# Two result buffers and a third for the last tile, with two-tile bodies, in a 2x2 average pool

## The chip, the cores and the metric

The kernel runs on one core of one Trainium2 chip. The metric is the device time of one execution in microseconds (us). Before the change it was 3103.94 us (median of six runs, 3103.81 to 3104.12). A program on one core has no second core or die to compare with.

## The reference

```python
# x: float32 [32, 128, 256, 256], kernel_size 2, stride 2 -> float32 [32, 128, 128, 128]
for i in range(h_out):
    for j in range(w_out):
        window = x[:, :, 2*i:2*i+2, 2*j:2*j+2]
        output[:, :, i, j] = np.mean(window, axis=(2, 3))
```

1.07 GB are read and 0.27 GB written, and there are three additions and one multiplication for each output.

## The kernel before

An output row is made of two neighbouring input rows, 512 numbers. A tile is 32 such pairs of rows on each of 128 partitions: 8 MB in (64 KB a partition), 2 MB out (16 KB a partition). There are 127 whole tiles, and one last tile that is cut into four parts (meant to keep the end of the run short). Four engines share the work:

- SyncE issues loads into two input buffers.
- VectorE adds the two rows of each pair (the first add, in place), then neighbouring columns (the second add, into a result buffer).
- ScalarE multiplies by 0.25 in place, tells SyncE that the input buffer is free, and issues the store.
- The DMA engines do the loads and stores.

Every dependence is a semaphore by hand. `take(engine, sem, n)` waits for `n` and takes it away again. The core of the program (cut; comments added here):

```python
TILE = 32
OUTS = 4
# ... ins: 2 tiles [128, 32, 512]; res: OUTS tiles [128, 32, 128]
def tile_sum(b, o, first=False):
    it, dst = ins[b], res[o]
    take(dve, loaded[b], 16)
    dve.tensor_add(out=it[:, :, 0:w], in0=it[:, :, 0:w], in1=it[:, :, w:]).then_inc(ready)
    if not first:
        take(dve, stored[o], 16)          # the store of four tiles back
    take(dve, ready)
    dve.tensor_add(out=dst, in0=it[:, :, 0:w:2], in1=it[:, :, 1:w:2]).then_inc(summed)

def tile_scale(b, o, done):
    take(act, summed)
    act.sem_inc(free[b])                  # SyncE may load into this input buffer
    act.mul(out=res[o], in_=res[o], mul=0.25).then_inc(done)

def tile_store(t, o):
    take(act, scaled)
    act.dma_start(out=ot[t], in_=res[o]).then_inc(stored[o], 16)
# ... the first four tiles of VectorE and ScalarE are written out, then a loop of four tiles a pass,
# ... then three tiles written out, then the four parts of the last tile
```

Of the kernel before, what the change touches and what calls it, by code (L numbers as in the profile page):

```python
# [9 lines left out]
@with_exitstack  # L10
def kernel(
    ctx: ExitStack,
    tc: tile.TileContext,
    x: bass.AP,
    kernel_size: bass.AP,
    stride: bass.AP,
    out: bass.AP,
):
    nc = tc.nc
    P = nc.NUM_PARTITIONS  # L20

    n, c, h, w = x.shape
    k = int(kernel_size)
    s = int(stride)
    h_out = (h - k) // s + 1
    w_out = (w - k) // s + 1
    R = n * c * h_out
    units = R // P if R % P == 0 else 0


    if k == 2 and s == 2 and h % 2 == 0 and w == 256 and units >= 1024:
        _pool_2x2(ctx, tc, x, out, units)
    else:
        _generic_pool(ctx, tc, x, out, k, s, n, c, h, w, h_out, w_out)


TILE = 32
OUTS = 4


def _pool_2x2(ctx, tc, x, out, units):
    nc = tc.nc
    P = nc.NUM_PARTITIONS
    f32 = mybir.dt.float32
    w = x.shape[3]
    w_out = w // 2
    sp, act, dve = nc.sync, nc.scalar, nc.vector

    xv = x.rearrange("n c (ho a) w -> (n c ho) (a w)", a=2)
    ov = out.rearrange("n c ho wo -> (n c ho) wo")  # L50

    in_pool = ctx.enter_context(tc.tile_pool(name="inp", bufs=2))
    out_pool = ctx.enter_context(tc.tile_pool(name="outp", bufs=OUTS))
    ins = [in_pool.tile([P, TILE, 2 * w], f32, name="in_tile") for _ in range(2)]
    res = [out_pool.tile([P, TILE, w_out], f32, name="res") for _ in range(OUTS)]

    loaded = [ctx.enter_context(nc.semaphore(f"loaded{b}")) for b in range(2)]
    free = [ctx.enter_context(nc.semaphore(f"free{b}")) for b in range(2)]
    summed = ctx.enter_context(nc.semaphore("summed"))
    scaled = ctx.enter_context(nc.semaphore("scaled"))  # L60
    stored = [ctx.enter_context(nc.semaphore(f"stored{b}")) for b in range(OUTS)]
    tail = ctx.enter_context(nc.semaphore("tail"))
    ready = ctx.enter_context(nc.semaphore("ready"))
    held = ctx.enter_context(nc.semaphore("held"))



    def take(engine, sem, n=1):
        engine.wait_ge(sem, n)
        engine.sem_inc(sem, -n)  # L70

    def block(r0, g):
        rows = slice(r0, r0 + g * P)
        return xv[rows].rearrange("(p g) f -> p g f", p=P), ov[rows].rearrange("(p g) f -> p g f", p=P)

    whole, rest = divmod(units - 1, TILE)
    rest += 1
    xt = xv[0:whole * TILE * P].rearrange("(t p g) f -> t p g f", p=P, g=TILE)
    ot = ov[0:whole * TILE * P].rearrange("(t p g) f -> t p g f", p=P, g=TILE)
    loops, left = divmod(whole - OUTS, OUTS)  # L80

    def tile_load(t, b):
        sp.dma_start(out=ins[b], in_=xt[t]).then_inc(loaded[b], 16)

    def tile_sum(b, o, first=False):
        it, dst = ins[b], res[o]
        take(dve, loaded[b], 16)
        dve.tensor_add(out=it[:, :, 0:w], in0=it[:, :, 0:w], in1=it[:, :, w:]).then_inc(ready)  # L88
        if not first:
            take(dve, stored[o], 16)  # L90
        take(dve, ready)
        dve.tensor_add(out=dst, in0=it[:, :, 0:w:2], in1=it[:, :, 1:w:2]).then_inc(summed)  # L92

    def tile_scale(b, o, done):
        take(act, summed)
        act.sem_inc(free[b])
        act.mul(out=res[o], in_=res[o], mul=0.25).then_inc(done)  # L97

    def tile_store(t, o):
        take(act, scaled)  # L100
        act.dma_start(out=ot[t], in_=res[o]).then_inc(stored[o], 16)

    parts, a = [], 0
    while a < rest:
        b = rest if rest - a <= 4 else a + (rest - a) // 2
        parts.append((a, b))
        a = b

    psem = [ctx.enter_context(nc.semaphore(f"part{k}")) for k in range(len(parts))]

    with tc.tile_critical():

        for b in range(2):
            tile_load(b, b)
        with sp.Fori(2, 2 + 2 * ((whole - 2) // 2), 2) as i:
            for b in range(2):
                take(sp, free[b])
                tile_load(i + b, b)
        t = 2 + 2 * ((whole - 2) // 2)
        while t < whole:  # L120
            take(sp, free[t % 2])
            tile_load(t, t % 2)
            t += 1



        take(sp, free[whole % 2])
        it, dst = ins[whole % 2], res[whole % OUTS]
        for (a, b), s in zip(parts, psem):
            sp.dma_start(out=it[:, a:b], in_=block((whole * TILE + a) * P, b - a)[0]).then_inc(s, 16)  # L130
        take(sp, held)
        sp.dma_start(out=ot[whole - 1], in_=res[(whole - 1) % OUTS]).then_inc(stored[(whole - 1) % OUTS], 16)


        for o in range(OUTS):
            tile_sum(o % 2, o, first=True)
        with dve.Fori(0, loops) as i:
            for o in range(OUTS):
                tile_sum(o % 2, o)
        for o in range(left):  # L140
            tile_sum(o % 2, o)
        take(dve, stored[whole % OUTS], 16)
        for (a, b), s in zip(parts, psem):
            take(dve, s, 16)
            dve.tensor_add(out=it[:, a:b, 0:w], in0=it[:, a:b, 0:w], in1=it[:, a:b, w:]).then_inc(ready)  # L145
            take(dve, ready)
            dve.tensor_add(out=dst[:, a:b], in0=it[:, a:b, 0:w:2], in1=it[:, a:b, 1:w:2]).then_inc(summed)  # L147


        for t in range(OUTS):  # L150
            tile_scale(t % 2, t, scaled)
            tile_store(t, t)
        with act.Fori(OUTS, OUTS + loops * OUTS, OUTS) as i:
            for o in range(OUTS):
                tile_scale(o % 2, o, scaled)
                tile_store(i + o, o)
        for t in range(OUTS + loops * OUTS, whole):
            tile_scale(t % 2, t % OUTS, scaled if t < whole - 1 else held)
            if t < whole - 1:
                tile_store(t, t % OUTS)  # L160
        act.sem_inc(free[(whole + 1) % 2], -1)
        for a, b in parts:
            take(act, summed)
            act.mul(out=dst[:, a:b], in_=dst[:, a:b], mul=0.25).then_inc(scaled)  # L164
            take(act, scaled)
            act.dma_start(out=block((whole * TILE + a) * P, b - a)[1], in_=dst[:, a:b]).then_inc(tail, 16)


        take(sp, tail, 16 * len(parts))
        for o in range(OUTS):  # L170
            if o != whole % OUTS:
                take(sp, stored[o], 16)


def _generic_pool(ctx, tc, x, out, k, s, n, c, h, w, h_out, w_out):
# [92 lines left out]
```

## Time and profile before

| | before |
|---|---|
| time, median of 6 | 3103.94 us |
| VectorE busy | 54% |
| ScalarE busy | 15% |
| DMA, 40 slices | nine tenths or more in each |
| moved over the span | 433 GB/s |

From the page of the kernel before: the DMA rows of its 40 slices, then the DMA queues (packets, MB, and the time that the packets took as a share of the span of 16 engines; q1 holds the loads, q10 the stores).

```profile
DMA  9999999999999999999999999999999999999999
GB/s 415 436 439 426 436 439 426 436 439 426 436 438 426 436 438 426 436 430 435 436 438 426 440 435 426 436 438 427 436 438 426 437 439 425 437 438 426 437 438 401
...
q1 hardware_dynamic: 19008, 1075.85, 80.1%
q10 hardware_dynamic: 18720, 266.35, 20.0%
```

The two shares add up to 100%: an engine always has a packet in hand. The packet records of the trace give 2.418 us to a load packet of 64 KB and 0.611 us to a store packet of 16 KB. A tile is eight of each on each engine, 8 x (2.418 + 0.611) = 24.2 us. That is the period of the kernel, and 128 of them are nearly the whole time.

From the same page, the costliest groups (line, engine, operation, output<-input, shapes, count | busy us in all, mean ns of one | idle time ahead of them and what ended it), and the DMA issues (KB each, median us from issue to landing).

```profile
L88 DVE TENSOR_TENSOR in_tile<-in_tile 128x8192 f32<-128x8192 f32 x127 | 1104.0, 8693 | 1395.9 <-DVEq L70 1395.9
L97 ACT ACTIVATE res<-res 128x4096 f32<-128x4096 f32 x127 | 459.2, 3616 | 2587.2 <-ACTq L70 2587.2
L92 DVE TENSOR_TENSOR res<-in_tile 128x4096 f32<-128x4096 f32 x127 | 562.0, 4425 | 18.6
...
out_dram<-res ACTq DMA_DIRECT2D x126, 2048.0 KB, 33.9
...
in_tile<-in_x_dram SPq DMA_DIRECT2D x127, 34.6
```

VectorE works 8.69 + 4.42 us on a tile and waits about 11 us ahead of the first add. "DVEq L70" is VectorE's own queue in `take`: the profile says that a semaphore was waited for, but not which. To know which, one must look up when each load and store landed. The trace keeps those semaphore updates, 16 for each transfer.

The timeline of the kernel before, in mid-run (start us, duration us, engine, line, operation; idle time ahead in brackets):

```profile
1519.59 8.69 DVE L88 TENSOR_TENSOR in_tile<-in_tile 128x8192 f32<-128x8192 f32 x1 [10.93 <-DVEq L70]
1528.43 4.42 DVE L92 TENSOR_TENSOR res<-in_tile 128x4096 f32<-128x4096 f32 x1
1533.05 3.62 ACT L97 ACTIVATE res<-res 128x4096 f32<-128x4096 f32 x1 [20.57 <-ACTq L70]
1536.91 0.34 ACTq L101 DMA_DIRECT2D out_dram<-res  x1
1543.77 8.69 DVE L88 TENSOR_TENSOR in_tile<-in_tile 128x8192 f32<-128x8192 f32 x1 [10.92 <-DVEq L70]
```

The first add at 1543.77 us belongs to tile 63, whose load landed at 1543.64 by the trace's semaphore updates: VectorE starts 0.13 us after its data.

### The profile page before, as it was taken

The page shows a single profiled execution, that of the slowest core. Times are in us where ns is not written, and L with a number is a line of the kernel's source. Part 1 is how long each engine was busy: PE and PEld are TensorE (multiplying, and loading weights), DVE is VectorE, ACT ScalarE, POOL GpSimd, SP SyncE. Part 2 cuts the span into 40 slices and gives each one's busy share as a digit, 9 for nine tenths or more (in the row PEclk, how much of TensorE's full clock was granted, in tenths as well). Part 3 has the DMA queues.
Part 4 walks back from the last instruction along what each step waited for, and adds up shares of the span by engine and source line. Part 5 has one row for each costly group of instructions (what it writes and reads, how often), then busy time and mean ns, then how long its engine had stood idle before and what let it go on. Part 6 is the DMA issues. An engine that isn't in the chain of part 4 may idle for free. (4 is left out here: it accounts for less than half of the span.)

```text
span 3103.1 us, 2444 instructions
## 1 busy us (share of the span) xinstructions
DVE 1679.7 (54%) x262; ACT 464.8 (15%) x132; POOL 0.2 (0%) x4
## 2 busy tenths in 40 slices
DVE  4555555555555555555555555555555555555555
ACT  1111111111111111111111111111111111111111
POOL 0000000000000000000000000000000000000000
DMA  9999999999999999999999999999999999999999
GB/s 415 436 439 426 436 439 426 436 439 426 436 438 426 436 438 426 436 430 435 436 438 426 440 435 426 436 438 427 436 438 426 437 439 425 437 438 426 437 438 401
DMA packets 37730, 1342.21 MB, mean 433 GB/s; under 512 B 4192, under 2 KB 4192, under 8 KB 4576
## 3 DMA queue, kind: packets, MB, share of 16 engines
q1 hardware_dynamic: 19008, 1075.85, 80.1%
q10 hardware_dynamic: 18720, 266.35, 20.0%
q14 instruction: 2, 0.02, 0.0%
HBM read 1073.74 MB, written 268.44 MB: 433 GB/s over the span
## 5 line engine op out<-in xcount | busy, mean ns | idle before, releaser
L88 DVE TENSOR_TENSOR in_tile<-in_tile 128x8192 f32<-128x8192 f32 x127 | 1104.0, 8693 | 1395.9 <-DVEq L70 1395.9
L97 ACT ACTIVATE res<-res 128x4096 f32<-128x4096 f32 x127 | 459.2, 3616 | 2587.2 <-ACTq L70 2587.2
L92 DVE TENSOR_TENSOR res<-in_tile 128x4096 f32<-128x4096 f32 x127 | 562.0, 4425 | 18.6
L145 DVE TENSOR_TENSOR in_tile<-in_tile 128x1024 f32<-128x1024 f32 (+2 forms) x4 | 9.1, 2287 | 1.3 <-DVEq L70 1.3
L97 ACT ACT_TABLE_LOAD x1 | 1.3, 1283 | 36.5 <-ACTq L70 36.5
L164 ACT ACTIVATE res<-res 128x512 f32<-128x512 f32 (+2 forms) x4 | 4.2, 1056 | 8.4 <-ACTq L70 8.4
L147 DVE TENSOR_TENSOR res<-in_tile 128x512 f32<-128x512 f32 (+2 forms) x4 | 4.9, 1225 | 0.6
L249 POOL MEMSET const-bfloat16-1.0<- 128x1 bf16 x1 | 0.1, 101 | 0.0
L249 POOL MEMSET const-uint8-127<- 128x1 uint8 x1 | 0.1, 101 | 0.0
L249 POOL MEMSET const-float32-0.0<- 128x1 f32 x1 | 0.1, 98 | 0.2 <-issue 0.2
L249 POOL MEMSET const-float32-1.0<- 128x1 f32 x1 | 0.1, 98 | 0.0
## 6 DMA issues: line engine op xcount, KB each, us to landing
out_dram<-res ACTq DMA_DIRECT2D x126, 2048.0 KB, 33.9
in_tile<-in_x_dram SPq DMA_DIRECT2D x1, 4096.0 KB, 25.1
in_tile<-in_x_dram SPq DMA_DIRECT2D x1, 2048.0 KB, 30.2
in_tile<-in_x_dram SPq DMA_DIRECT2D x2, 1024.0 KB, 33.2
out_dram<-res SPq DMA_DIRECT2D x1, 2048.0 KB, 13.8
in_tile<-in_x_dram SPq DMA_DIRECT2D x127, 34.6
out_dram<-res ACTq DMA_DIRECT2D x1, 1024.0 KB, 7.4
out_dram<-res ACTq DMA_DIRECT2D x1, 512.0 KB, 5.4
```

Of the source, the lines that this page charges most:

```text
L88: dve.tensor_add(out=it[:, :, 0:w], in0=it[:, :, 0:w], in1=it[:, :, w:]).then_inc(ready)
L92: dve.tensor_add(out=dst, in0=it[:, :, 0:w:2], in1=it[:, :, 1:w:2]).then_inc(summed)
L97: act.mul(out=res[o], in_=res[o], mul=0.25).then_inc(done)
L145: dve.tensor_add(out=it[:, a:b, 0:w], in0=it[:, a:b, 0:w], in1=it[:, a:b, w:]).then_inc(ready)
L147: dve.tensor_add(out=dst[:, a:b], in0=it[:, a:b, 0:w:2], in1=it[:, a:b, 1:w:2]).then_inc(summed)
L164: act.mul(out=dst[:, a:b], in_=dst[:, a:b], mul=0.25).then_inc(scaled)
L249: nc = _bacc.Bacc("TRN2", target_bir_lowering=False, num_devices=1)
```

## The change

The change makes the program smaller: the bodies of the loops hold two tiles instead of four, and nothing is written out ahead of VectorE's loop. For that the result buffers go from four to two, with a third for the last tile alone. The last stores share one semaphore. The wait for the store moves ahead of the first add.

The core of the diff (cut):

```diff
-OUTS = 4
...
-    out_pool = ctx.enter_context(tc.tile_pool(name="outp", bufs=OUTS))
+    out_pool = ctx.enter_context(tc.tile_pool(name="outp", bufs=3))
...
-    def tile_sum(b, o, first=False):
-        it, dst = ins[b], res[o]
-        take(dve, loaded[b], 16)
-        dve.tensor_add(out=it[:, :, 0:w], in0=it[:, :, 0:w], in1=it[:, :, w:]).then_inc(ready)
-        if not first:
-            take(dve, stored[o], 16)
-        take(dve, ready)
-        dve.tensor_add(out=dst, in0=it[:, :, 0:w:2], in1=it[:, :, 1:w:2]).then_inc(summed)
+    def sums(it, dst):
+        dve.tensor_add(out=it[:, :, 0:w], in0=it[:, :, 0:w], in1=it[:, :, w:]).then_inc(halfway)
+        take(dve, halfway)
+        dve.tensor_add(out=dst, in0=it[:, :, 0:w:2], in1=it[:, :, 1:w:2]).then_inc(summed)
+
+    def tile_sums(b):
+        take(dve, stored[b], 16)          # now the store of TWO tiles back, and ahead of the first add
+        take(dve, loaded[b], 16)
+        sums(ins[b], res[b])
...
-        with dve.Fori(0, loops) as i:
-            for o in range(OUTS):
-                tile_sum(o % 2, o)
+        for b in range(2):
+            dve.sem_inc(stored[b], 16)
+        with dve.Fori(0, whole // 2):
+            for b in range(2):
+                tile_sums(b)
...
-        take(sp, tail, 16 * len(parts))
-        for o in range(OUTS):
-            if o != whole % OUTS:
-                take(sp, stored[o], 16)
+        take(sp, tail, 16 * (len(parts) + 2))
```

(The comment on the wait is added here.)

More of the change, by code (lines that the diff above doesn't have):

```diff
@@ L52, in _pool_2x2, with sem @@
     in_pool = ctx.enter_context(tc.tile_pool(name="inp", bufs=2))
-    out_pool = ctx.enter_context(tc.tile_pool(name="outp", bufs=OUTS))
+    out_pool = ctx.enter_context(tc.tile_pool(name="outp", bufs=3))
     ins = [in_pool.tile([P, TILE, 2 * w], f32, name="in_tile") for _ in range(2)]
-    res = [out_pool.tile([P, TILE, w_out], f32, name="res") for _ in range(OUTS)]
-    loaded = [ctx.enter_context(nc.semaphore(f"loaded{b}")) for b in range(2)]
-    free = [ctx.enter_context(nc.semaphore(f"free{b}")) for b in range(2)]
-    summed = ctx.enter_context(nc.semaphore("summed"))
-    scaled = ctx.enter_context(nc.semaphore("scaled"))
-    stored = [ctx.enter_context(nc.semaphore(f"stored{b}")) for b in range(OUTS)]
-    tail = ctx.enter_context(nc.semaphore("tail"))
-    ready = ctx.enter_context(nc.semaphore("ready"))
-    held = ctx.enter_context(nc.semaphore("held"))
+    res = [out_pool.tile([P, TILE, w_out], f32, name="res") for _ in range(3)]
+    def sem(name):
+        return ctx.enter_context(nc.semaphore(name))
+    loaded, free, stored = [[sem(f"{n}{b}") for b in range(2)] for n in ("loaded", "free", "stored")]
+    halfway, summed, scaled, held, tail = [sem(n) for n in ("halfway", "summed", "scaled", "held", "tail")]
     def take(engine, sem, n=1):
@@ L79, in _pool_2x2 @@
     ot = ov[0:whole * TILE * P].rearrange("(t p g) f -> t p g f", p=P, g=TILE)
-    loops, left = divmod(whole - OUTS, OUTS)
-    def tile_load(t, b):
-        sp.dma_start(out=ins[b], in_=xt[t]).then_inc(loaded[b], 16)
-    def tile_sum(b, o, first=False):
-        it, dst = ins[b], res[o]
-        take(dve, loaded[b], 16)
-        dve.tensor_add(out=it[:, :, 0:w], in0=it[:, :, 0:w], in1=it[:, :, w:]).then_inc(ready)
-        if not first:
-            take(dve, stored[o], 16)
-        take(dve, ready)
-        dve.tensor_add(out=dst, in0=it[:, :, 0:w:2], in1=it[:, :, 1:w:2]).then_inc(summed)
-    def tile_scale(b, o, done):
-        take(act, summed)
-        act.sem_inc(free[b])
-        act.mul(out=res[o], in_=res[o], mul=0.25).then_inc(done)
-    def tile_store(t, o):
-        take(act, scaled)
-        act.dma_start(out=ot[t], in_=res[o]).then_inc(stored[o], 16)
     parts, a = [], 0
@@ L105, in _pool_2x2, with load @@
         b = rest if rest - a <= 4 else a + (rest - a) // 2
-        parts.append((a, b))
+        parts.append((a, b, sem(f"part{len(parts)}")))
         a = b
-    psem = [ctx.enter_context(nc.semaphore(f"part{k}")) for k in range(len(parts))]
+    def load(t, b):
+        sp.dma_start(out=ins[b], in_=xt[t]).then_inc(loaded[b], 16)
+    def sums(it, dst):
+        dve.tensor_add(out=it[:, :, 0:w], in0=it[:, :, 0:w], in1=it[:, :, w:]).then_inc(halfway)
+        take(dve, halfway)
+        dve.tensor_add(out=dst, in0=it[:, :, 0:w:2], in1=it[:, :, 1:w:2]).then_inc(summed)
@@ L111, in _pool_2x2, with scale, scale_store @@
+    def tile_sums(b):
+        take(dve, stored[b], 16)
+        take(dve, loaded[b], 16)
+        sums(ins[b], res[b])
+    def scale(dst, done=scaled):
+        act.mul(out=dst, in_=dst, mul=0.25).then_inc(done)
+    def scale_store(t, b, landed):
+        take(act, summed)
+        act.sem_inc(free[b])
+        scale(res[b])
+        take(act, scaled)
+        act.dma_start(out=ot[t], in_=res[b]).then_inc(landed, 16)
     with tc.tile_critical():
-        for b in range(2):
-            tile_load(b, b)
@@ L115, in _pool_2x2 @@
-        with sp.Fori(2, 2 + 2 * ((whole - 2) // 2), 2) as i:
+        load(0, 0)
+        load(1, 1)
+        pairs = (whole - 2) // 2
+        with sp.Fori(2, 2 + 2 * pairs, 2) as i:
             for b in range(2):
                 take(sp, free[b])
-                tile_load(i + b, b)
-        t = 2 + 2 * ((whole - 2) // 2)
-        while t < whole:
+                load(i + b, b)
+        for t in range(2 + 2 * pairs, whole):
             take(sp, free[t % 2])
-            tile_load(t, t % 2)
-            t += 1
+            load(t, t % 2)
@@ L127, in _pool_2x2 @@
         take(sp, free[whole % 2])
-        it, dst = ins[whole % 2], res[whole % OUTS]
-        for (a, b), s in zip(parts, psem):
-            sp.dma_start(out=it[:, a:b], in_=block((whole * TILE + a) * P, b - a)[0]).then_inc(s, 16)
+        it, dst = ins[whole % 2], res[2]
+        for a, b, part in parts:
+            sp.dma_start(out=it[:, a:b], in_=block((whole * TILE + a) * P, b - a)[0]).then_inc(part, 16)
         take(sp, held)
-        sp.dma_start(out=ot[whole - 1], in_=res[(whole - 1) % OUTS]).then_inc(stored[(whole - 1) % OUTS], 16)
@@ L135, in _pool_2x2 @@
-        for o in range(OUTS):
-            tile_sum(o % 2, o, first=True)
-        with dve.Fori(0, loops) as i:
-            for o in range(OUTS):
-                tile_sum(o % 2, o)
-        for o in range(left):
-            tile_sum(o % 2, o)
-        take(dve, stored[whole % OUTS], 16)
-        for (a, b), s in zip(parts, psem):
-            take(dve, s, 16)
-            dve.tensor_add(out=it[:, a:b, 0:w], in0=it[:, a:b, 0:w], in1=it[:, a:b, w:]).then_inc(ready)
-            take(dve, ready)
-            dve.tensor_add(out=dst[:, a:b], in0=it[:, a:b, 0:w:2], in1=it[:, a:b, 1:w:2]).then_inc(summed)
@@ L150, in _pool_2x2 @@
-        for t in range(OUTS):
-            tile_scale(t % 2, t, scaled)
-            tile_store(t, t)
-        with act.Fori(OUTS, OUTS + loops * OUTS, OUTS) as i:
-            for o in range(OUTS):
-                tile_scale(o % 2, o, scaled)
-                tile_store(i + o, o)
-        for t in range(OUTS + loops * OUTS, whole):
-            tile_scale(t % 2, t % OUTS, scaled if t < whole - 1 else held)
-            if t < whole - 1:
-                tile_store(t, t % OUTS)
-        act.sem_inc(free[(whole + 1) % 2], -1)
@@ L162, in _pool_2x2 @@
-        for a, b in parts:
+        sp.dma_start(out=ot[whole - 1], in_=res[(whole - 1) % 2]).then_inc(tail, 16)
+        for b in range(2):
[3 more added lines that the diff above has]
+                tile_sums(b)
+        if whole % 2:
+            tile_sums(0)
+        for a, b, part in parts:
+            take(dve, part, 16)
+            sums(it[:, a:b], dst[:, a:b])
+        scale_store(0, 0, stored[0])
+        pairs = (whole - 3) // 2
@@ L163, in _pool_2x2 @@
+        with act.Fori(1, 1 + 2 * pairs, 2) as i:
+            for b in (1, 0):
+                scale_store(i + 1 - b, b, stored[b])
+        for t in range(1 + 2 * pairs, whole - 1):
+            scale_store(t, t % 2, stored[t % 2] if t < whole - 2 else tail)
+        take(act, summed)
+        scale(res[(whole - 1) % 2], held)
+        for a, b, _ in parts:
             take(act, summed)
-            act.mul(out=dst[:, a:b], in_=dst[:, a:b], mul=0.25).then_inc(scaled)
+            scale(dst[:, a:b])
@@ L165, in _pool_2x2 @@
             take(act, scaled)
             act.dma_start(out=block((whole * TILE + a) * P, b - a)[1], in_=dst[:, a:b]).then_inc(tail, 16)
-        take(sp, tail, 16 * len(parts))
-        for o in range(OUTS):
-            if o != whole % OUTS:
-                take(sp, stored[o], 16)
+        take(sp, tail, 16 * (len(parts) + 2))
 def _generic_pool(ctx, tc, x, out, k, s, n, c, h, w, h_out, w_out):
```

## The prediction

> **What bounds it now.** The profile's first part shows VectorE 54% busy and ScalarE 15%, while the row of 40 slices shows the DMA engines at nine tenths or more throughout, at 433 GB/s over the span. The packets say the same: a load packet (64 KB) takes 2.418 us and a store packet (16 KB) 0.611 us, 27.1 and 26.8 GB/s on each of 16 engines; a tile is 8 of each per engine, 8 x 3.029 = 24.2 us, and the timeline's period is 24.18 us. The kernel is a full DMA pipe. [...]
>
> **What the change does.** The bytes, packets, and vector and scalar work (8.69 + 4.42 + 3.62 us a tile) stay. Two-tile bodies earn nothing, since no sequencer was late. Only one dependence is new: two result buffers instead of four, and the wait for the store two tiles back now comes before the FIRST add. In the trace that store lands after the load which starts the tile: load of tile 2 at 68.59 us, store 0 at 71.61; tile 64's load 1567.82, store 62 at 1570.83; tile 65's 1591.99 and 1594.99. So I expect each first add 3.0 us later than its load, from tile 2 on.
>
> **Why that should be nearly free.** [...] Load t+2 is issued when tile t is summed: at 1508.9 us, while the load in flight begins to land on its fastest engines at 1517.05, 8.2 us of room, which becomes 5.2. The store is issued at 1512.7 while the previous one begins to land at 1520.1: 7.4 us becomes 4.4. An issue takes about 2 us to start (the last small store: issued 3096.97, first landing 3099.54, with 0.65 us of data). Both queues stay filled. If one did run dry, the other would get the engines: [...] the trace shows loads and stores alternating one for one. So landings should not move; the delay doesn't accumulate, as stores still land every 24.18 us.
>
> **On the critical path** only the tail. Tile 126's first add waits for store 124 (3068.86) instead of its load (3067.05): +1.8 us. Its sums then end at 3082.2 instead of 3080.4; the first part of the last tile started at 3081.73, so that chain moves about +0.5 us. The last engine is busy with stores to 3101.49 without a gap and may hide even this. Sum: +0.2 us[...].
>
> **Predicted: 3104.0 us, 8 in 10 between 3102.8 and 3106.0. Chances: faster by over 2% 0.5%, within 2% 98.5%, slower by over 2% 1%.**
>
> **What would show it.** Idle before the first add from 10.9 to 13.9 us in mid-run, its wait total from 1396 to about 1770 us; store issue-to-landing from 33.9 to about 31 us, load's from 34.6 to about 31.6; DMA still at nine tenths in every slice; period still 24.18 us.
>
> **What would make it wrong.** If the later issues find a queue empty and engines idle, each tile loses: 1 us a tile is 125 us (4%). If one engine's lag (it lands 2.4 us after the others from tile 2 on, and ends 2.4 us after most of them) disappears or grows, up to 2.5 us either way.

(The sum is the +0.2 us of the tail, by which 3103.94 us become 3104.1; the forecast's middle is 3104.0. For "no sequencer was late", the trace of the kernel before has the first add 0.13 us after its load, a load issued 0.35 us after the second add's end, and a store 0.1 to 0.25 us after the scaling.)

## The result, and the profile after

| | before | after |
|---|---|---|
| time, median of 6 | 3103.94 us (3103.81 to 3104.12) | 3103.55 us (3103.25 to 3103.70) |
| ratio | | 0.9999, 95% interval 0.9986 to 1.0011 |
| store, issue to landing | 33.9 us | 30.8 us |
| load, issue to landing | 34.6 us | 31.5 us |

The ratio is the mean time of one kernel's fast runs over that of the other's of the same rounds, so it is not quite the ratio of the medians. The verdict is the same time, as predicted (3104.0 us, 3102.8 to 3106.0).

The same lines of the page after:

```profile
DMA  9999999999999999999999999999999999999999
GB/s 416 436 440 426 436 440 426 437 440 424 438 440 423 439 437 425 440 428 434 440 433 430 442 423 436 439 427 440 435 426 437 439 427 436 438 424 439 437 425 416
...
q1 hardware_dynamic: 19008, 1075.85, 80.1%
q10 hardware_dynamic: 18720, 266.35, 20.1%
...
L87 DVE TENSOR_TENSOR in_tile<-in_tile 128x8192 f32<-128x8192 f32 (+1 forms) x131 | 1113.0, 8496 | 1396.4 <-DVEq L67 1396.4
...
out_dram<-res ACTq DMA_DIRECT2D x126, 2048.0 KB, 30.8
...
in_tile<-in_x_dram SPq DMA_DIRECT2D x127, 31.5
```

The group L87 now holds the parts of the last tile too, so its count is 131. The total of VectorE's wait is unchanged: 1396.4 us against 1395.9. The prediction had said 1770. The timeline after, at the same place, shows why that figure was a mistake:

```profile
1520.94 8.69 DVE L87 TENSOR_TENSOR in_tile<-in_tile 128x8192 f32<-128x8192 f32 x1 [10.93 <-DVEq L67]
1529.78 4.43 DVE L89 TENSOR_TENSOR res<-in_tile 128x4096 f32<-128x4096 f32 x1
1534.39 3.62 ACT L97 ACTIVATE res<-res 128x4096 f32<-128x4096 f32 x1 [20.58 <-ACTq L67]
1538.24 0.34 ACTq L104 DMA_DIRECT2D out_dram<-res  x1
1545.13 8.69 DVE L87 TENSOR_TENSOR in_tile<-in_tile 128x8192 f32<-128x8192 f32 x1 [10.93 <-DVEq L67]
```

Tile 63's load landed at 1541.86 us here, and its first add begins at 1545.13, 3.27 us later (0.13 before). So the new wait is there: by the trace's semaphore updates, first adds begin 3.20 to 3.29 us after their loads in all of tiles 2 to 125, and 2.07 us after in tile 126. But the period is still 24.2 us and the work in it still 13.2 us, so the idle time in it is still 10.9 us. A delay that is the same in every tile shifts VectorE once. It shows as idle time in one tile only, the first that meets it.

The landings were 1.8 us earlier in this profile (1541.86 against 1543.64), mostly for another reason, below: in the profile before, one of the 16 engines lagged by 2.39 us (0.99 us between the first and the last engine here), and VectorE starts only after the slowest. In the trace before, tile 2's load made 15 of its 16 updates within 0.63 us, the last came 2.40 us after the first, and VectorE started 0.13 us after that one.

### The profile page after: what moved, and what is told of

Read it like the earlier page. It is cut to its first block, busy times and chain, and to the rows that moved or that the text cites. A ratio compares the mean times of both kernels' runs of the same rounds, so it can differ in the third digit from the quotient of the medians.

```text
span 3101.5 us, 2614 instructions
## 1 busy us (share of the span) xinstructions
DVE 1679.6 (54%) x262; ACT 464.7 (15%) x132; POOL 0.2 (0%) x4
## 3 DMA queue, kind: packets, MB, share of 16 engines
q1 hardware_dynamic: 19008, 1075.85, 80.1%
q10 hardware_dynamic: 18720, 266.35, 20.1%
## 5 line engine op out<-in xcount | busy, mean ns | idle before, releaser
L87 DVE TENSOR_TENSOR in_tile<-in_tile 128x8192 f32<-128x8192 f32 (+1 forms) x131 | 1113.0, 8496 | 1396.4 <-DVEq L67 1396.4
L97 ACT ACTIVATE res<-res 128x4096 f32<-128x4096 f32 (+1 forms) x131 | 463.5, 3538 | 2594.8 <-ACTq L67 2594.8
L89 DVE TENSOR_TENSOR res<-in_tile 128x4096 f32<-128x4096 f32 (+1 forms) x131 | 566.8, 4327 | 19.2
## 6 DMA issues: line engine op xcount, KB each, us to landing
out_dram<-res ACTq DMA_DIRECT2D x126, 2048.0 KB, 30.8
in_tile<-in_x_dram SPq DMA_DIRECT2D x127, 31.5
```

The costliest lines, as they stand in the source:

```text
L97: act.mul(out=dst, in_=dst, mul=0.25).then_inc(done)
```

## The experiments

Two theories stood at the start. *Full pipe*: the DMA engines never run dry, the wait only shifts VectorE, and nothing was paid. *Paid and repaid*: the wait costs something, and shorter programs or the third buffer gave it back. The first four runs (five rounds each, on one chip, with nine runs of the kernel before, median 3104.01 us) test these. Of the next four, three were to find where the room ends, and one whether wider stores save time; their results changed the theory, and the last four settle the changed one. The last four ran on another chip, on which the kernel before took 3103.98 us, against 3103.97 and 3104.01 on the first. All twelve gave correct results.

### The kernel before again (no edit)

> The kernel before, unchanged: a null run, for the noise and for the one engine that lagged by 2.39 us in the profile before (0.39 us, later 1.2 us, in the profile after). If that lag belongs to the program, it is 2.4 us again from tile 2 on and the profiled span is 3103.1 us again; if it is an accident of one execution, it differs, and the span moves with it by 1 to 2 us. Time: 3104.0 us, within 0.3 us.

Measured: 3104.01 us (3103.72 to 3104.08), profiled span 3102.0 us. The lag was 0.41 us at tile 2 and 1.47 us at the end. The lag thus differs between executions of one program, and the 3103.1 us span of the first profile was an unlucky one.

### The changed kernel again (no edit)

> The changed kernel, unchanged. Full-pipe theory (the DMA engines never run dry, the new wait only shifts VectorE): 3103.6 us, within 0.3 us of that; first add of tile 2 again some 3.2 us after its load has landed; last engine's lag again small or different. If the 0.4 us by which the six runs after lay below the six before are real, this run lies below the null run by 0.2 to 0.6 us; if not, the two overlap.

Measured: 3103.51 us (3103.36 to 3103.69), ratio 0.9998 (0.9984 to 1.0012), profiled span 3101.7 us. These two runs form a fair pair of profiles, since their lags are alike (0.41 and 0.47 us at tile 2). Here are the first add of tile 2 and the issue of the last store in the timeline of the null run:

```profile
66.49 8.69 DVE L88 TENSOR_TENSOR in_tile<-in_tile 128x8192 f32<-128x8192 f32 x1 [10.86 <-DVEq L70]
...
3095.79 0.34 ACTq L166 DMA_DIRECT2D out_dram<-res  x1
```

and in that of the changed kernel:

```profile
69.80 8.69 DVE L87 TENSOR_TENSOR in_tile<-in_tile 128x8192 f32<-128x8192 f32 x1 [14.29 <-DVEq L67]
...
3096.22 0.34 ACTq L154 DMA_DIRECT2D out_dram<-res  x1
```

Tile 2 is the one tile with the extra idle time: 14.29 us instead of 10.86. Its load landed at 66.54 us in the changed kernel, and store 0, which it now waits for, at 69.55. At the end, the last store is issued 0.43 us later; the prediction had worked out 0.5. The time does not show even that.

### Two buffers, and nothing else

```diff
-OUTS = 4
+OUTS = 2
```

> The kernel before with the number of result buffers alone changed, 4 to 2; the wait for the store stays between the two adds. Full-pipe theory: the store of two tiles back lands about 3 us into a first add of 8.69 us, so the wait never bites, VectorE starts 0.13 us after its load as before, and the time is that of before within 0.5 us, plus up to 1.2 us at the end because the last tile now waits for the store of tile 125. Rival (the second buffer pair bought something, and the change paid for it elsewhere): slower by several us, up to 3 us a tile, 380 us in all.

Measured: 3103.68 us (3103.36 to 3104.01), ratio 0.9998. Store issue to landing stayed at 34.0 us, so the wait between the adds does not bite. As foreseen, the last tile waits for the store of tile 125, and the last store is issued at 3097.17 us, 1.38 us later than in the null run. The time did not rise by it: the last two stores landed 3.9 us after their issue (median) instead of 5.2, so the later issue did not move the landings, and the DMA row of this run's page is at nine tenths in its last slice too. The rival's 380 us are not there.

### The changed kernel with the wait between the adds

```diff
     def sums(it, dst, before_second=None):
         dve.tensor_add(... first add ...)
+        if before_second is not None:
+            take(dve, before_second, 16)
         take(dve, halfway)
 ...
-        take(dve, stored[b], 16)
         take(dve, loaded[b], 16)
-        sums(ins[b], res[b])
+        sums(ins[b], res[b], stored[b])
```

> The changed kernel with the wait for the store moved back between the two adds; all else as changed. Full-pipe theory: the first add starts 0.13 us after its load again, stores are issued 3 us earlier, store issue to landing back from 30.8 to about 34 us, and the time stays within 0.5 us of 3103.6. Rival (the early wait costs, and the shorter programs or the third buffer pay it back): faster than the changed kernel by what the wait costs, 1 us or more, up to 380 us if the 3 us counted in every tile.

Measured: 3103.49 us (3103.32 to 3103.68), ratio 0.9998. Store issue to landing is back at 33.9 us: the shift is gone. The time is that of the changed kernel to 0.02 us. So the early wait costs nothing that these runs can see, and there is nothing to repay. *Paid and repaid* falls.

### One more add on VectorE

The edit, without the lines that make `scratch` and `padded` (comment added here):

```diff
         take(dve, stored[b], 16)
         take(dve, loaded[b], 16)
+        for _ in range(1):     # into a buffer that nobody reads
+            dve.tensor_add(out=scratch, in0=ins[b][:, :, 0:w:2], in1=ins[b][:, :, 1:w:2]).then_inc(padded)
+            take(dve, padded)
         sums(ins[b], res[b])
```

> The changed kernel with one more add of 4.42 us on VectorE in every tile, ahead of the first, into a buffer nobody reads (about 4.6 us with its wait; results unchanged). Full-pipe theory: the room between the issue of a load and the landing of the one in flight was 8.2 us before, 5.2 us changed, less some 2 us for an issue to start; 4.6 us more uses it up, but the store queue still holds work, so the time stays within 0.3% (3103 to 3113 us). Rival (delays on VectorE reach the time, and the change was repaid elsewhere): 4.6 us in each of 127 tiles, 3690 us.

Measured: 3289.56 us (3275.03 to 3293.62), ratio 1.058. Both expectations miss: not 3103 to 3113, and not 3690. The 4.6 us are more than the room that the prediction counted (5.2 and 4.4 us, each less about 2), so this run does not refute the count itself; what fails is that the other queue fills the hole. From this run's page:

```profile
DMA  9999999999999999999999999999999999999999
GB/s 416 400 408 407 409 417 406 413 407 401 415 412 405 410 397 417 412 405 408 399 421 406 417 411 398 415 397 405 408 407 408 407 409 408 398 414 414 405 419 384
...
q1 hardware_dynamic: 19008, 1075.85, 78.5%
q10 hardware_dynamic: 18720, 266.35, 18.9%
```

The row of nines looks as before, with 6% lost. The GB/s row and the queues show it: 78.5 + 18.9 = 97.4% of 3290.9 us, so the engines were idle for 2.6%, 85 us, and their packets took 3206 us in all instead of the changed kernel's 3106, 100 us more. Together that is 185 of the 189 us between the two spans (3290.9 and 3101.5 us). The mean load packet took 2.517 us instead of 2.419; of the 16256, 9394 still took 2.418 us and 1392 took 3.0 us or more. And its timeline (`x2` stands for two issues, from the start of the first to the end of the second):

```profile
1511.05 4.42 DVE L100 TENSOR_TENSOR scratch<-in_tile 128x4096 f32<-128x4096 f32 x1 [13.59 <-DVEq L70]
1515.62 8.69 DVE L90 TENSOR_TENSOR in_tile<-in_tile 128x8192 f32<-128x8192 f32 x1
1524.46 4.42 DVE L92 TENSOR_TENSOR res<-in_tile 128x4096 f32<-128x4096 f32 x1
1529.07 3.62 ACT L105 ACTIVATE res<-res 128x4096 f32<-128x4096 f32 x1 [27.80 <-ACTq L70]
1529.24 19.72 SPq L87 DMA_DIRECT2D in_tile<-in_x_dram  x2
1530.44 4.42 DVE L100 TENSOR_TENSOR scratch<-in_tile 128x4096 f32<-128x4096 f32 x1 [1.56 <-DVEq L70]
1532.92 0.34 ACTq L112 DMA_DIRECT2D out_dram<-res  x1
```

Tiles no longer come evenly: one waits 13.59 us, the next follows 1.56 us behind, and two take 51 us instead of 48.4. The load at 1529.24 is issued when the pipe has just emptied. Counted from the packet records, the engines were busy 51% of the us from 1529 and 55% of the us from 1530, and fully again from 1531. All 16 engines then start a load packet between 1530.2 and 1531.0 us, and no store packet starts before 1538.4: loads have the engines to themselves. But the first three load packets of each engine take 3.02, 2.43 and 2.66 us on average, not 2.418. At the start of the run one sees how it comes about: store 0 lands at 75.69 us and tile 2's load at 69.70, so tile 2 now waits 6 us for a store, not 3; its sums end late, and by then both the load ahead (93.88) and the store ahead (95.09) have landed or nearly so.

### Two more adds

> The same with two more adds, about 9.1 us: VectorE then works 22.4 us of each tile's 24.2. Full-pipe theory: the load queue now runs dry on the fast engines before the next load arrives. If the store queue fills the hole each time, still within 0.5% of 3104 us; if both queues run dry, DMA drops below nine tenths and the time rises by 1 to 4% (3130 to 3230 us). This run finds where the room ends. Rival (each us on VectorE counts): 4260 us.

(The edit is that of the run above, with `range(2)`.) Measured: 3499.41 us (3490.77 to 3531.01), ratio 1.131. Again above the range. The DMA row falls to eights in 15 of its 40 slices.

### One result buffer

The edit, cut (`sums` and `scale` also use `res[0]`):

```diff
-        take(dve, stored[b], 16)
+        take(dve, stored[1 - b], 16)      # the store of the tile before
 ...
-        act.dma_start(out=ot[t], in_=res[b]).then_inc(landed, 16)
+        act.dma_start(out=ot[t], in_=res[0]).then_inc(landed, 16)
```

> The changed kernel with one result buffer instead of two (the last tile keeps its own): each tile's first add waits for the store of the tile before. Full-pipe theory says that this must break the pipe: 13.3 us of adds, 3.9 us of scaling and issue, then a store of 7 us (alone) to 24 us (one for one with loads) before the next tile: 26 to 41 us a tile, 3300 to 5200 us, with DMA below nine tenths. If it should stay at 3104 us, result buffers don't matter at all and the theory of room is wrong.

(The 7 and 24 us of a store are estimates from the packet times above: 8 x 0.611 us and about 2 us to start, and 8 x 3.029 us. Stores took 23.9 us here, the median from issue to landing.)

Measured: 5313.35 us (5306.81 to 5322.34), ratio 1.712, just above the range. With the wait ahead of the first add one buffer is too few: a tile takes 41.4 us, and the DMA row falls to fives and sixes after its first slice. The prediction's first sentence on danger ("if the later issues find a queue empty ... each tile loses") is what this run and the two before it show.

### Stores of two tiles

The result buffers hold two tiles, and a store moves 32 KB a partition in one piece (in short, not the literal lines):

```diff
-    ins, res: 2 x [128, 32, 512], 3 x [128, 32, 128]
+    ins, res: 2 x [128, 32, 512], 2 x [128, 64, 128]
-    xt = xv[...].rearrange("(t p g) f -> t p g f", p=P, g=TILE)
+    xt = xv[...].rearrange("(t p h g) f -> t h p g f", p=P, h=2, g=TILE)   # two loads
+    ot = ov[...].rearrange("(t p g) f -> t p g f", p=P, g=2 * TILE)        # one store
```

> Not a test of the change but of what is left above the DMA: result buffers of two tiles each, one store for two tiles, so that a store packet is 32 KB (1.213 us in the traces) instead of 16 KB (0.611 us). 0.009 us less for each of 504 pairs of packets on an engine: 4.5 us. Full-pipe theory: about 3099 us, if rows 64 KB apart in every load cost nothing; stores share one for one with loads by packet, so they land sooner (about 30 us for twice the bytes). If packet time isn't what bounds the kernel, 3104 us or more.

Measured: 3155.34 us (3146.91 to 3180.28), ratio 1.019 (1.0142 to 1.0238): slower, though whether by 2% is unclear. A miss: the stores took 33.7 us from issue to landing (median), not about 30; the store packets did take 1.214 us, but the mean load packet took 2.463 us instead of 2.419, and 1016 of them on an engine are 45 us. Whether the cause is the distance between the rows of a load (it moves 64 KB of each 128 KB) or the bunched stores, this run does not tell apart. It is left open. The 16 updates of a load came apart here: in mid-run they are spread over 2.5 and 3.7 us, about 1.0 us in the changed kernel.

### The theory after these eight

A load can be issued when its buffer is summed (0.35 us after it in the trace of the kernel before); a store when the result is scaled (0.1 to 0.25 us after it). If VectorE is late, both are. With the wait of the change there is a second path: a late store delays the first add of two tiles later, which delays the next store and load again. In the kernel before that path has far more room: the store is that of four tiles back, and only the second add waits for it. If this is right, the kernel before must bear the extra add that costs the changed one 186 us; and the changed kernel must bear it when the wait stands between the adds. If the number of buffers counts, or the two input buffers, they must lose as much.

### The kernel before with one more add

```diff
         take(dve, loaded[b], 16)
+        for _ in range(1):
+            dve.tensor_add(out=scratch, in0=it[:, 0:31, 0:w:2], in1=it[:, 0:31, 1:w:2]).then_inc(padded)
+            take(dve, padded)
```

> The kernel before (four result buffers, wait between the adds) with the extra add of the run that came out at 3290 us on the changed kernel (31 of its 32 rows, 4.3 us[...]). Theory now: that loss came from the early wait on the store two tiles back, which turns a late store into a late first add, a later store and a later load, until both DMA queues run dry for 2 us in every second tile. Without that wait only the room between loads counts (8.2 us less about 2 us to start), so 4.4 us is free: 3103 to 3108 us. Rival: the room between loads itself was under 4.4 us, and any kernel with two input buffers loses as much: about 3280 us.

Measured: 3105.24 us (3104.83 to 3106.71), ratio 1.0005 (0.9989 to 1.0022). The extra add costs 1.3 us in all, inside the interval. Its timeline:

```profile
1512.16 24.53 SPq L86 DMA_DIRECT2D in_tile<-in_x_dram  x2
1515.87 0.34 ACTq L107 DMA_DIRECT2D out_dram<-res  x1
1518.30 4.29 DVE L92 TENSOR_TENSOR scratch<-in_tile 128x3968 f32<-128x3968 f32 x1 [6.49 <-DVEq L73]
1522.74 8.69 DVE L94 TENSOR_TENSOR in_tile<-in_tile 128x8192 f32<-128x8192 f32 x1
1531.58 4.43 DVE L98 TENSOR_TENSOR res<-in_tile 128x4096 f32<-128x4096 f32 x1
```

The idle time shrinks from 10.9 to 6.5 us and takes the add up. Tiles still come every 24.2 us.

### The changed kernel with one more add and the wait between the adds

> The changed kernel with the extra add AND the wait for the store moved back between the two adds; still two result buffers and the third for the last tile. If the place of the wait is what costs, the store has 13 us more to land and the wait never bites: 3103 to 3108 us. If the number of buffers is what costs, wherever the wait stands: near 3290 us.

(The edit is that of the wait moved back and that of one more add, together.) Measured: 3105.07 us (3104.97 to 3105.17), ratio 1.0003. Against 3289.56 us this run differs in the place of one wait alone. The page shows full queues again:

```profile
q1 hardware_dynamic: 19008, 1075.85, 80.1%
q10 hardware_dynamic: 18720, 266.35, 20.1%
```

So with two buffers it is the place of the wait that costs: moved back, two buffers bear the extra add as well as four do. Nor does the add's own work on the chip make packets longer: the mean load packet took 2.420 us here. Four buffers with the early wait were not run.

### Half of the extra add

> The changed kernel with half of the extra add (16 of 32 rows, 2.29 us, 2.4 us with its wait). The store was issued 4.4 us before the one ahead of it lands, less about 2 us to start, so 2.4 us is just the end of the room: 3103 to 3115 us if room is what it is about, with first adds 5 us or more after their loads. If the loss grows in proportion to what is added (186 us for 4.6 us), about 3200 us.

(The edit is that of one more add, on 16 of the 32 rows.) Measured: 3129.58 us (3127.05 to 3136.55), ratio 1.0087 (1.007 to 1.0104): under 2%, but clear of the noise. It is between the two expectations, and outside both: the room of the changed kernel ends below 2.4 us. Its page:

```profile
DMA  9999999999999999999999999999999999999999
...
q1 hardware_dynamic: 19008, 1075.85, 80.2%
q10 hardware_dynamic: 18720, 266.35, 19.9%
```

The shares add up to 100.1%, as they did before. No engine idles, and yet 26 us are lost. They went into longer packets: the mean load packet took 2.444 us against 2.419, and the sum of what is over 2.418 us is 26.8 us on an engine, against 1.2 us in the changed kernel. The difference, 25.6 us, is nearly the whole loss of 26.0 (spans of 3127.5 and 3101.5 us). A store's 16 updates are now spread over 4.6 us (1603.49 to 1608.08 for store 63; about 1.0 us in the changed kernel), so the engines drift apart, and the early wait waits for the last of them. Longer packets and drift come together; which of them brings the other, and how, no run here shows.

### The kernel before with two more adds

> The kernel before with two extra adds (2 x 4.4 us; VectorE works about 22.1 us of a tile's 24.2). On the changed kernel two cost 395 us. Theory: only the room between loads counts here, and 8.8 us is over it by some 2.5 us; the store queue, which with four buffers is not empty then, covers part: 3106 to 3200 us, well below 3499. Rival (room is the same with four buffers): about 3490 us.

Measured: 3291.32 us (3284.92 to 3298.50), ratio 1.060: above the range, far below the rival's 3490. The room of the kernel before is between 4.4 and 8.9 us. Its page:

```profile
q1 hardware_dynamic: 19008, 1075.85, 80.3%
q10 hardware_dynamic: 18720, 266.35, 18.9%
```

Here 80.3 + 18.9 = 99.2% of 3290.9 us are packets: 26 us of idle engines, and 159 us of longer packets (mean load packet 2.575 us).

All together (medians in us; added time with its wait):

| added to VectorE in each tile | 4 buffers, wait between the adds (before) | 2 + 1 buffers, wait between the adds | 2 + 1 buffers, wait first (the change) |
|---|---|---|---|
| nothing | 3103.94 | 3103.49 | 3103.55 |
| 2.4 us | | | 3129.58 |
| 4.4 to 4.6 us | 3105.24 | 3105.07 | 3289.56 |
| 8.9 to 9.1 us | 3291.32 | | 3499.41 |

The change costs no time. It used up room that the kernel had against a late VectorE: 4.4 us more in each tile cost the kernel before 1.3 us in all, and 2.4 us more cost the changed one 26.

## Why the prediction was right, and which steps of it were not

- **"The kernel is a full DMA pipe"; the bytes and packets stay.** Right. The queues' shares are 80.1 and 20.1% after, at 433 GB/s, and the period is 24.2 us.
- **"Each first add 3.0 us later than its load, from tile 2 on."** Right: 3.26 us at tile 2 and 3.27 us in mid-run (3.0 us for the store, 0.25 us for two waits in a row). Moving the wait back takes the shift away and changes the time by 0.02 us (3103.49 against 3103.51 us on the same chip).
- **Issue to landing 31 and 31.6 us.** Right: 30.8 and 31.5. Both fall by the shift, since issues move and landings don't.
- **"Idle before the first add from 10.9 to 13.9 us, its wait total from 1396 to about 1770."** Wrong: 10.93 us and 1396.4 us. A constant delay is a shift of phase, and only tile 2 shows it (14.29 us in place of 10.86 in the pair of alike profiles).
- **"On the critical path only the tail ... about +0.5 us", +0.2 in the sum.** The last issue did move by +0.43 us in the pair. The time didn't follow; with two buffers alone the last issue moved by 1.38 us and the time did not follow either. The +0.2 was thus nothing.
- **"5.2 us" and "4.4 us" of room, less about 2.** Too large, though the result did not depend on it: that leaves 3.2 and 2.4 us, and with 2.4 us more the time had already risen by 26 us, so the room ends before that; where, no run measured. The sum left out that the new wait couples stores to loads, which the two runs with 4.6 us more and the wait in either place show, 3105.07 against 3289.56 us. That the 3.0 us of the change still fitted was to that extent luck.
- **"If one did run dry, the other would get the engines."** It does, but this does not save the time: with one more add the loads got all 16 engines at 1530 us, and their packets took longer (3.02 us for the first); with half an add the engines were always busy and the packets were slower. The turn-taking is in the trace of the kernel before: on an engine a 64 KB load packet (2.418 us), a 16 KB store packet (0.611 us), and so on, one for one. That it keeps the rate up was a conclusion of the prediction, and the 2.444 us packets refute it.
- **0.4 us.** The changed kernel's medians (3103.55, 3103.51, and 3103.49 with the wait moved) lie 0.4 to 0.5 us below those of before (3103.94, 3104.01), and two buffers alone lie between (3103.68). The intervals of the ratios reach about 4 us to either side. It isn't the early wait. The first profile before and the null run each show two instruction fetches of 8 KB within the run, at about 3040 and 3090 us, and the profiles of the changed kernel, of the wait moved and of two buffers alone show none; that shorter programs earn these tenths is a guess that no run tests.

## What to carry to other kernels

In this kernel, whose DMA engines had packets for 100% of the span, a new wait on VectorE that made each load and store issue about 3 us later took no time (3103.55 us after, 3103.94 before), but 2.4 us of work on top of it took 26 us. So measure how much later issues could be by adding known work, because the time alone does not show how much of that room a change has used. Put the wait for a buffer right before the instruction that writes the buffer, not ahead of work that doesn't need it: here both places took the same time, but with 4.6 us more work the early one lost 184 us that the late one did not. And don't read a constant delay off the idle column: here it showed once (14.29 us in place of 10.86 in tile 2), then it was only a shift (10.9 us in mid-run, before and after).
